# Two RMS norms of a decoder block: their sums over partitions taken by 32x32 block turns on VectorE instead of by products with ones

## The chip, the cores and the metric

The kernel runs on one core of a Trainium2 chip. The metric is the time of one execution in microseconds (us). The engines that matter here: PE (TensorE, matrix products; PEld is its loading of weights), DVE (VectorE), ACT (ScalarE), POOL (GpSimd) and SP (SyncE, which here only issues DMAs). All engines run on their own and in program order, and wait for each other by semaphores.

## What is computed

One decoder block over 256 tokens with a model width of 1024. Two of its steps are RMS norms over the width, one ahead of the attention part and one ahead of the gated feed-forward part (FFN). The reference, cut to that:

```python
def rms_norm(x, g):
    y = x * lax.rsqrt(jnp.mean(x * x, axis=-1, keepdims=True) + NORM_EPS)
    return y * g

h = rms_norm(x, attn_norm_g)
proj = jnp.einsum('bsd,de->bse', h, w_in)       # q, k, v of two attentions, forget, gates
...                                             # MoBA and FoX attention, gated merge
x = x + jnp.einsum('bsd,de->bse', merged, w_out)
h2 = rms_norm(x, ffn_norm_g)
up = jnp.einsum('bsd,df->bsf', h2, w_ffn_up)    # 1024 -> 2 x 2816
u, g = jnp.split(up, 2, axis=-1)
g = causal_depthwise_conv(g, ffn_conv_w, ffn_conv_b)
x = x + jnp.einsum('bsf,fd->bsd', jax.nn.silu(g) * u, w_ffn_down)
```

## The kernel before, in words

**Layout.** x lies transposed: the width on partitions (8 tiles of 128), the 256 tokens along the free axis. A norm therefore needs a sum over partitions. The gain g is multiplied into x early; the factor 1/sqrt(mean square) of a token is a scale of the result, so it is applied to what the products leave in PSUM. No product waits for it; what reads PSUM does.

**Three products for one.** Every large product is made in fp32r with both operands split into a high and a low part: hi*hi, lo*hi and hi*lo. ACT writes the high part of a weight (tile `whi`), DVE the low part (`wlo`); `load` records both for one "unit", which is half of a 1 MB weight chunk. SP fetches the chunks into `raw`, three buffers deep: a chunk's load is issued once DVE has made both low parts of the chunk three before it. PE uses the units in a fixed order; the splits run some five units ahead (six buffers each of `whi` and `wlo`).

**What sets the order.** PE's order is that of the code. For the other engines a scheduler sets it at build time from priorities (`soon`) and from extra orderings that `after` adds. A DMA that SP or POOL issues runs on the same 16 DMA engines.

**First norm.** ACT squares the tiles of x, POOL adds them up into `xss`, and `norm1_sums` splits the sum in two and multiplies it with a matrix of ones (two matmuls, L251), which leaves each token's sum on all partitions. `norm1` picks the diagonal (L257), works out the factor on 128x2 elements (`rsqrt_mean`, L228 to L232: DVE, ACT twice, DVE three times), turns it to rows (L262) and has POOL write those to DRAM and read them back spread over all partitions as `rsB` (L265, L266). The factor by token (`rs`) scales q, k and v; `rsB` scales the gates (L561).

**Second norm.** While the product with w_out ends (L680 to L682), DVE adds the residual (L685), ACT squares (L691), and POOL adds up `sqs` (L693 to L696). ACT and POOL split `sqs` (L700, L701). The function `norm2` stands inside `up(1)`, between matmuls: two products with ones (L714, L715) leave the sum of each token on all 128 partitions, and `rsqrt_mean` works out the factor `rs2` on 128x256 elements, already where it is used.

**FFN.** `up(f)` makes 48 matmuls of u and g of one 128-wide slice f into one of the eight PSUM banks. `finish_up(f)` reads it with `rs2` (L723), then convolution (ACT L727, DVE L728 and L729), SiLU (ACT L730), product with u (DVE L733) and the split for the next product (ACT L737, DVE L738) into `qT`, `kT` or `aT` by turns. `down(p)` multiplies slices 2p and 2p+1 with w_down. PE's order is up(0), up(1), up(2), up(3), down(0), up(4), up(5), down(1) and so on. `down` holds five banks from its first use to the end.

Of the kernel before, what the change touches and what calls it, by code (L numbers as in the profile page):

```python
# [8 lines left out]
F32 = mybir.dt.float32  # L9
# [3 lines left out]
ALU = mybir.AluOpType  # L13
# [31 lines left out]
def decoder_block(ctx, tc, a, out):  # L45
# [7 lines left out]
    def T(shape, tag, bufs=1, dt=F32):  # L53
        return sb.tile(shape, dt, tag=tag, bufs=bufs, name=tag)
# [4 lines left out]
    def bank():  # L59
        return ps.tile([P, 512], F32, tag="bank", bufs=8, name="bank")  # L60
# [33 lines left out]
    split = {}  # L94
    loads = {}
    rs_done = []
    first_lo = []
    state = {"next": 0, "raw": None, "lag": 0, "hi": None, "lo": None}

    def after(i, j):  # L100
# [2 lines left out]
    def load(upto):  # L103
        while state["next"] <= min(upto, len(units) - 1):
            c, h = units[state["next"]]
            if c[0] == "head":
                k = c[1]
                if k < 2:
                    raw = gates[:, 4 * k:4 * k + 4].rearrange("p a b t -> p (a b t)")
                    for s0, s1 in ((0, HX + W4), (HX + W4, HEADW)):  # L110
                        loads[c] = nc.sync.dma_start(raw[:, s0:s1], a["head"][k][:, s0:s1])
                    x, g, raw = raw[:, 0:S], raw[:, S:S + 1], raw[:, HX:HEADW]
                    nc.gpsimd.tensor_copy(xT[:, k], x)
                else:
                    if k % 2 == 0:
                        state["raw"] = T([P, 2048], "raw", RB)
                    raw = state["raw"][:, k % 2 * 1024:(k % 2 + 1) * 1024]
                    x, g = xT[:, k], g1[:, k:k + 1]
                    nc.sync.dma_start(x, a["head"][k][:, 0:S])
                    loads[c] = nc.sync.dma_start(raw, a["head"][k][:, HX:HEADW])  # L120
                xlo = split_x(k, x, g)
                at, n = 44, 2 if k < 2 else 1
            else:
                at, n = 44 if c[0] == "qkv" else 0, 1
                if h == 0:
                    src = a[c[0]]
                    for j in c[1:]:
                        src = src[j]
                    state["raw"] = T([P, 2048], "raw", RB)
                    loads[c] = nc.sync.dma_start(state["raw"], src)  # L130
                raw = state["raw"][:, h * 1024:(h + 1) * 1024]
            hi = T([P, 1088], "whi", HB, F32R)[:, at:at + 1024]
            lo = T([P, 1088], "wlo", HB, F32R)[:, at:at + 1024]
            w = 1024 // n
            for j in range(n):
                s = slice(j * w, (j + 1) * w)
                i = nc.scalar.activation(hi[:, s], raw[:, s], AF.Copy)  # L137
                d = nc.vector.tensor_tensor(lo[:, s], raw[:, s], hi[:, s].bitcast(F32), op=ALU.subtract)  # L138
                if (c, h) == (("qkv", 1, 1), 0):
                    after(i, rs_done[0])  # L140
                    after(d, rs_done[1])
                if (c, h) == (("qkv", 1, 0), 0):
                    first_lo.append(d)
                if c[0] == "head" and j == 0:
                    after(d, xlo)
                for this, last in ((i, state["hi"]), (d, state["lo"])):
                    if last is not None:
                        after(this, last)
            if c[0] == "head":
                square_x(k, x, i)  # L150
            split[c, h] = (hi, lo)
            state["last"] = i, d
            state["next"] += 1
# [49 lines left out]
    load(5)  # L203
    cst = T([P, 840], "cst")
    ident = cst[:, 0:128]
    ones = cst[:, 256:384]
    mask3 = cst[:, 384:768]
    cos2 = cst[:, 768:832].rearrange("p (t c) -> p t c", t=NT)
    sel = cst[:, 832:840]
    wfr = T([P, KT, NH], "wfr")  # L210
    wfg = T([P, KT, 32], "wfg")
    nc.gpsimd.memset(wfg, 0.0)
    gq = T([P, 2], "gq")

    casts = []

    def tables():
        for t, n in ((sm, "smalls"), (cst, "consts"), (wfr, "wf")):
            after(nc.sync.dma_start(t, a[n]), loads["head", KT - 1])
        nc.gpsimd.memset(first_ones.bitcast(F32), 1.0)  # L220
        nc.vector.tensor_scalar_mul(gq, sm[:, C_QG:C_QG + 4:2], -HD ** -0.5)
        nc.vector.tensor_tensor(wfg[:, :, 0:NH], wfr, g1[:, :, None].to_broadcast([P, KT, NH]), op=ALU.mult)

    def rsqrt_mean(dst, ss, n, shape, tag, bufs=2):

        w = T([P, 3] + shape, tag, bufs)
        v, y, t = w[:, 0], w[:, 1], w[:, 2]
        nc.vector.tensor_scalar(v, ss, 1.0 / n, EPS, op0=ALU.mult, op1=ALU.add)  # L228
        i = nc.scalar.activation(t, v, AF.Ln), nc.scalar.activation(y, t, AF.Exp, scale=-0.5)
        nc.vector.scalar_tensor_tensor(t, v, -0.5, y, op0=ALU.mult, op1=ALU.mult)  # L230
        nc.vector.tensor_tensor(t, t, y, op=ALU.mult)
        d = nc.vector.scalar_tensor_tensor(dst, t, 1.5, y, op0=ALU.add, op1=ALU.mult)  # L232
        return i + (d,)

    rsw = T([P, 32], "rsw")
    nc.gpsimd.memset(rsw, 0.0)
    rs = rsw[:, 0:NT]
    rsB = T([P, S], "rsB")
    rope = []
    flat = T16(4, "aT")  # L240

    first_ones = flat[:, 3, P:2 * P]

    def norm1_sums():
        nc.scalar.activation(flat[:, 0], xss[:, 1], AF.Copy)
        low = nc.gpsimd.tensor_tensor(flat[:, 1], xss[:, 1], flat[:, 0].bitcast(F32), op=ALU.subtract)
        for i in casts:
            after(i, low)
        ssp = wp[:, 0:S]
        for i in range(2):  # L250
            nc.tensor.matmul(ssp, first_ones, flat[:, i], start=(i == 0), stop=(i == 1))  # L251
        return ssp

    def norm1(ssp):
        ss1 = T([P, NT], "ss1")
        for t in range(NT):
            i = nc.vector.tensor_tensor_reduce(T([P, 512], "sq", 2)[:, 0:P], ssp[:, t * P:(t + 1) * P], ident, scale=1.0, scalar=0.0,  # L257
                                               op0=ALU.mult, op1=ALU.add, accum_out=ss1[:, t:t + 1])
            after(i, first_lo[0])
        rs_done.extend(rsqrt_mean(rs, ss1, D, [NT], "rsv")[1:])  # L260
        rsT = T([P, 32], "rsT")
        nc.vector.transpose(rsT, rsw)  # L262
        rd = dr.tile([NT, P], F32, name="rd")
        for t in range(NT):
            nc.gpsimd.dma_start(rd[t].rearrange("(i p) -> i p", p=32), rsT[t:P:32])  # L265
        nc.gpsimd.dma_start(rsB, bass.AP(tensor=rd.tensor, offset=rd.offset, ap=[[0, P], [1, S]]))  # L266

        for i in range(2):
            gr = sm[:, C_GR + 16 * i:C_GR + 16 * (i + 1)][:, None, :].to_broadcast([P, NT, 16])
            rc = T([P, NT, 16], f"rc{i}")  # L270
            rsn = T([P, NT, 16], f"rsn{i}")
            nc.vector.tensor_tensor(rc, cos2[:, :, 0:16], gr, op=ALU.mult)
            nc.vector.tensor_tensor(rsn, cos2[:, :, 16:32], gr, op=ALU.mult)
            rope.append((rc, rsn))
# [304 lines left out]
    for k in range(KT):  # L579
        if k == KT - 1:  # L580
            with soon():
                ssp = norm1_sums()
                norm1(ssp)
        project_qk(k, (pq, pk))
        if k == 2:
            tables()
# [84 lines left out]
    for c in range(4):  # L671
        for h in range(2):
# [10 lines left out]
            if c >= 2:  # L683
# [8 lines left out]
                if j == 0:  # L692
                    nc.gpsimd.tensor_tensor(sqs, sq[:, 0], sq[:, 1], op=ALU.add)  # L693
                else:
                    nc.gpsimd.tensor_tensor(sqs, sqs, sq[:, 0], op=ALU.add)
                    nc.gpsimd.tensor_tensor(sqs, sqs, sq[:, 1], op=ALU.add)  # L696
    sqr = T([P, NH, 384], "bias", 1, F32R)
    sqh, sql, ones_r = sqr[:, 0, 0:S], sqr[:, 1, 0:S], sqr[:, 2, 0:P]
    nc.gpsimd.tensor_copy(ones_r, ones)
    nc.scalar.activation(sqh, sqs, AF.Copy)  # L700
    nc.gpsimd.tensor_tensor(sql, sqs, sqh.bitcast(F32), op=ALU.subtract)  # L701
    sp = bank()
    rs2 = T([P, S], "rs2")


    acts = {}

    def up(f):
        up_ = bank()
        twin("wu", f, up_, hh, hl, f == 0, norm2 if f == 1 else None)  # L710
        return up_

    def norm2():
        nc.tensor.matmul(sp[:, 0:S], ones_r, sqh, start=True, stop=False)  # L714
        nc.tensor.matmul(sp[:, 0:S], ones_r, sql, start=False, stop=True)  # L715
        i = rsqrt_mean(rs2, sp[:, 0:S], D, [S], "s", 4)
        after(i[0], tables[0])
        tables.append(nc.scalar.preload_act_table_set("silu_and_others"))
        after(tables[1], i[1])

    def finish_up(f, up_):
        ev = T([P, 2, S], "sq", 2)
# [121 lines left out]
```

## Time and profile before

| | before |
|---|---|
| time, median of 3 runs | 360.86 us (360.52 to 361.11) |
| the profiled execution | 361.65 us, of which the span from first to last instruction is 359.9 us |
| mean granted TensorE clock | 0.997 |
| DVE, ACT, POOL busy | 75%, 62%, 11% of the span |
| HBM read | 66.75 MB, 188 GB/s over the span |

In a group's row stand line, engine, operation, tiles written<-read, shape, count, and after the bar the busy time and the mean of one in ns. In a timeline's row stand the start and the length in us, then engine, line and operation; behind it in brackets the engine's idle time before it and what ended that. A PE row's length includes the pipeline's depth; the distance of two starts is what a matmul takes of PE.

### The profile page before, as it was taken

To read this page: it belongs to the slowest core of one execution; us is meant where nothing else is said; L and a number is where in the kernel's file an instruction comes from. 1 tells how busy PE (TensorE), PEld (TensorE's weight loads), DVE (VectorE), ACT (ScalarE), POOL (GpSimd) and SP (SyncE) were. 2 spreads that over 40 slices of the span, in tenths; PEclk is the share of its full clock that TensorE was granted. 3 is DMA by queue.
4 is the path that set the end of the run, shared out by engine and by line. 5 is a ranking of instruction groups with operands and counts; after the bars stand their busy time and mean duration, and the time that the engine had idled before them with its cause. 6 is when DMAs were issued, how large, how long until landed. Compare 5 with 4: busy or idle time off the path is not lost.

```text
span 359.9 us, 7545 instructions
## 1 busy us (share of the span) xinstructions
PE 354.6 (99%) x3117; PEld 337.9 (94%) x3117; DVE 271.0 (75%) x463; ACT 221.5 (62%) x376; POOL 39.9 (11%) x54
## 2 busy tenths in 40 slices
PE   9999999999999999999999999999999999999995
PEld 5888899888899999999999999999999999999995
DVE  5899669798995558875969776868676776768643
ACT  5859656799894995545877654555464555555420
POOL 2442051430410000000530000000000000000000
PEclk9999999999999999999999999999999999999998
DMA  8986634557348335565464564564564564563003
GB/s 270 403 323 236 207 158 176 178 219 250 117 136 335 118 118 177 181 229 201 152 228 168 192 235 164 188 233 153 201 232 157 198 229 138 217 211 143 0 2 117
DMA packets 12130, 68.28 MB, mean 190 GB/s; under 512 B 1688, under 2 KB 2848, under 8 KB 4672
## 3 DMA queue, kind: packets, MB, share of 16 engines
q1 hardware_dynamic: 11664, 66.62, 51.4%
q0 software_dynamic: 288, 1.19, 0.8%
q8 instruction: 24, 0.39, 0.4%
q14 instruction: 10, 0.08, 0.1%
q10 hardware_dynamic: 144, 0.00, 0.0%
HBM read 66.75 MB, written 1.06 MB: 188 GB/s over the span
## 4 chain that ended last, share of the span: by engine, by line
PE 99%; issue 0%; DVE 0%
PE bank L551 15%; PE bank L552 15%; PE bank L553 15%; PE bank L299 12%; PE bank L285 6%; PE bank L757 6%; PE bank L758 6%; PE bank L756 6%; PE bank L682 2%; PE bank L656 2%; PE bank L681 2%; PE bank L680 2%; PE bank L655 2%; PE bank L654 2%; PE bank L520 1%; PE bank L445 1%
## 5 line engine op out<-in xcount | busy, mean ns | idle before, releaser
L138 DVE TENSOR_TENSOR wlo<-raw,whi 128x1024 fp32r<-128x1024 f32 x120 | 147.1, 1232 | 46.1 <-ACT whi L137 46.0
L137 ACT ACTIVATE whi<-raw 128x1024 fp32r<-128x1024 f32 x120 | 125.5, 1058 | 67.5 <-PE bank L552 39.5
L553 PE MATMUL bank<-oh,wlo 128*128 128x256 f32 x352 | 96.8, 275 | 0.0
L551 PE MATMUL bank<-oh,whi 128*128 128x256 f32 x352 | 96.8, 275 | 0.0
L552 PE MATMUL bank<-ol,whi 128*128 128x256 f32 x352 | 96.8, 275 | 0.0
L551 PEld LDWEIGHTS bank<-oh,whi 128*128 128x128 f32 x352 | 66.1, 188 | 0.0
L552 PEld LDWEIGHTS bank<-ol,whi 128*128 128x128 f32 x352 | 66.1, 188 | 0.0
L553 PEld LDWEIGHTS bank<-oh,wlo 128*128 128x128 f32 x352 | 66.1, 188 | 0.0
L552 PE MATMUL bank<-xl,whi 128*128 128x256 f32 x128 | 35.4, 276 | 0.4 <-issue 0.4
L551 PE MATMUL bank<-xh,whi 128*128 128x256 f32 x128 | 35.6, 278 | 0.0
L553 PE MATMUL bank<-xh,wlo 128*128 128x256 f32 x128 | 35.3, 276 | 0.0
L552 PEld LDWEIGHTS bank<-xl,whi 128*128 128x128 f32 x128 | 24.0, 188 | 0.8 <-issue 0.6
L551 PEld LDWEIGHTS bank<-xh,whi 128*128 128x128 f32 x128 | 24.0, 188 | 0.3
L553 PEld LDWEIGHTS bank<-xh,wlo 128*128 128x128 f32 x128 | 24.0, 188 | 0.0
L299 PE MATMUL bank<-whi,xh 128*128 128x512 f32 x64 | 21.2, 391 | 0.0
L299 PE MATMUL bank<-wlo,xh 128*128 128x512 f32 x64 | 21.0, 388 | 0.0
L299 PE MATMUL bank<-whi,xl 128*128 128x512 f32 x64 | 20.9, 388 | 0.0
L723 DVE TENSOR_TENSOR sq<-bank,rs 128x512 f32<-128x512 f32 x22 | 15.1, 691 | 6.6 <-PE bank L553 6.5
L654 PE MATMUL bank<-oh,whi 128*128 128x256 f32 x64 | 17.6, 275 | 0.0
L655 PE MATMUL bank<-ol,whi 128*128 128x256 f32 x64 | 17.6, 275 | 0.0
L656 PE MATMUL bank<-oh,wlo 128*128 128x256 f32 x64 | 17.6, 275 | 0.0
L680 PE MATMUL bank<-xh,whi 128*128 128x256 f32 x64 | 17.6, 275 | 0.0
(197 smaller groups left out, 754.6 us busy)
## 6 DMA issues: line engine op xcount, KB each, us to landing
raw<-in_wu SPq DMA_DIRECT2D x22, 1024.0 KB, 4.8
raw<-in_wd SPq DMA_DIRECT2D x11, 1024.0 KB, 4.8
raw<-in_qkv SPq DMA_DIRECT2D x8, 1024.0 KB, 5.1
raw<-in_wg SPq DMA_DIRECT2D x8, 1024.0 KB, 5.0
raw<-in_wb SPq DMA_DIRECT2D x4, 1024.0 KB, 4.9
raw<-in_wo SPq DMA_DIRECT2D x4, 1024.0 KB, 4.8
raw<-in_head SPq DMA_DIRECT2D x6, 512.0 KB, 6.6
gates<-cd POOLq DMA_DIRECT2D x1, 1024.0 KB, 6.9
```

Source lines behind the costliest of these rows:

```text
L137: i = nc.scalar.activation(hi[:, s], raw[:, s], AF.Copy)
L138: d = nc.vector.tensor_tensor(lo[:, s], raw[:, s], hi[:, s].bitcast(F32), op=ALU.subtract)
L285: nc.tensor.matmul(pt[t], lhs[:, k, t * P:(t + 1) * P], rhs, start=(k == 0 and i == 0), stop=(k == KT - 1 and i == 2))
L299: nc.tensor.matmul(pt[t], lhs[:, k, t * P:(t + 1) * P], rhs[:, c], start=(k == 0 and i == 0), stop=(k == KT - 1 and i == 2))
L551: nc.tensor.matmul(o, wh[:, w], mh[:, k], start=(k == 0 and i == 0), stop=False)
L552: nc.tensor.matmul(o, wh[:, w], ml[:, k], start=False, stop=False)
L553: nc.tensor.matmul(o, wl[:, w], mh[:, k], start=False, stop=(k == KT - 1 and i == 1))
L654: nc.tensor.matmul(o, wh[:, w], oh[:, 4 * br + k], start=(k == 0), stop=False)
L655: nc.tensor.matmul(o, wh[:, w], ol[:, 4 * br + k], start=False, stop=False)
L656: nc.tensor.matmul(o, wl[:, w], oh[:, 4 * br + k], start=False, stop=(k == 3))
L680: nc.tensor.matmul(o, wh[:, w], mh[:, k], start=(k == 0 and i == 0), stop=False)
L756: nc.tensor.matmul(o, wh[:, w], ah, start=(p == 0 and h == 0 and c == 0), stop=False)
```

## The change

Both norms get a new function `token_norm`. It turns the 128x256 sum in blocks of 32x32 on DVE (`turned`), so that tokens lie on partitions within each block; reduces over 32 (`part`, 128x8); copies the four groups of 32 partitions side by side (`four`, four copies of 32x8); reduces over the four (`total`, 32x8); works out the factor on 32x8; turns it to rows (`rows`); and has POOL write them to DRAM and read them back over all partitions. The matmuls with ones and the splits ahead of them go. In the first norm four more copies bring the factor into `rs`. In the second the last two additions into `sqs` move from POOL to DVE, the row `rs2` comes by way of DRAM, and the code stands ahead of `up(0)` instead of inside `up(1)`.

```diff
-    def norm1_sums():
-        nc.scalar.activation(flat[:, 0], xss[:, 1], AF.Copy)
-        low = nc.gpsimd.tensor_tensor(flat[:, 1], xss[:, 1], flat[:, 0].bitcast(F32), op=ALU.subtract)
-        ssp = wp[:, 0:S]
-        for i in range(2):
-            nc.tensor.matmul(ssp, first_ones, flat[:, i], start=(i == 0), stop=(i == 1))
-        return ssp
...
+    def token_norm(xx, row):
+        turned = T([P, S], "turned")
+        nc.vector.transpose(turned, xx)
+        part = T([P, NH], "part")
+        nc.vector.tensor_reduce(part, turned.rearrange("p (b t) -> p b t", t=32), axis=AX.X, op=ALU.add)
+        four = T([32, NH, 4], "four")
+        for q in range(4):
+            nc.vector.tensor_copy(four[:, :, q], part[32 * q:32 * (q + 1)])
+        total = T([32, NH], "total")
+        nc.vector.tensor_reduce(total, four, axis=AX.X, op=ALU.add)
+        i = rsqrt_mean(rst[:, 0:NH], total, D, [NH], "rsv", rows=32)
+        rows = T([32, 32], "rows")
+        nc.vector.transpose(rows, rst)
+        rd = dr.tile([NH, 32], F32, name="rd")
+        nc.gpsimd.dma_start(rd, rows[0:NH])
+        nc.gpsimd.dma_start(row, bass.AP(tensor=rd.tensor, offset=rd.offset, ap=[[0, P], [1, S]]))
+        return i
...
+    def norm1():
+        i = token_norm(xss[:, 1], rsB)
+        for q in range(4):
+            d = nc.vector.tensor_copy(rs[32 * q:32 * (q + 1)], rst[:, q:NH:4])
+        rs_done.extend((i[1], d))
...
-                    nc.gpsimd.tensor_tensor(sqs, sqs, sq[:, 0], op=ALU.add)
-                    nc.gpsimd.tensor_tensor(sqs, sqs, sq[:, 1], op=ALU.add)
-    sqr = T([P, NH, 384], "bias", 1, F32R)
-    sqh, sql, ones_r = sqr[:, 0, 0:S], sqr[:, 1, 0:S], sqr[:, 2, 0:P]
-    nc.gpsimd.tensor_copy(ones_r, ones)
-    nc.scalar.activation(sqh, sqs, AF.Copy)
-    nc.gpsimd.tensor_tensor(sql, sqs, sqh.bitcast(F32), op=ALU.subtract)
-    sp = bank()
+                    for b in range(2):
+                        (nc.vector if j == 3 else nc.gpsimd).tensor_tensor(sqs, sqs, sq[:, b], op=ALU.add)
     rs2 = T([P, S], "rs2")
+    i = token_norm(sqs, rs2)
+    after(i[0], tables[0])
+    tables.append(nc.scalar.preload_act_table_set("silu_and_others"))
+    after(tables[1], i[1])
...
-    def norm2():
-        nc.tensor.matmul(sp[:, 0:S], ones_r, sqh, start=True, stop=False)
-        nc.tensor.matmul(sp[:, 0:S], ones_r, sql, start=False, stop=True)
-        i = rsqrt_mean(rs2, sp[:, 0:S], D, [S], "s", 4)
```

Line numbers in the program after are lower by 1 to 22 for the same code. On DVE at the first norm the rows before are these; the two low parts (`wlo`) belong to the two units that PE takes up first after the head chunks:

```order
L138 TENSOR_TENSOR wlo<-raw,whi 128x1024
L257 ISA sq,ss_320<-bank,cst 128x128
L257 ISA ss_320 128x1
L257 ISA sq,ss_320<-bank,cst 128x128
L257 ISA ss_320 128x1
L138 TENSOR_TENSOR wlo<-raw,whi 128x1024
L228 TENSOR_SCALAR rsv<-ss_320 128x2
L230 SCALAR_TENSOR_TENSOR rsv<-rsv 128x2
L231 TENSOR_TENSOR rsv<-rsv 128x2
L232 SCALAR_TENSOR_TENSOR rsw<-rsv 128x2
L262 STREAM_TRANSPOSE rsT<-rsw 128x32
```

In the program after, both stand behind the whole norm, and two small products for the rotation (`rc`, `rsn`) between its steps:

```order
L237 COPY four<-part 32x8 x4
L261 TENSOR_TENSOR rc_346<-cst,sm 128x32
L262 TENSOR_TENSOR rsn_347<-cst,sm 128x32
L239 TENSOR_REDUCE total<-four 32x8
L220 TENSOR_SCALAR rsv<-total 32x8
L222 SCALAR_TENSOR_TENSOR rsv<-rsv 32x8
L223 TENSOR_TENSOR rsv<-rsv 32x8
L224 SCALAR_TENSOR_TENSOR rst<-rsv 32x8
L242 STREAM_TRANSPOSE rows<-rst 32x32
L254 COPY rs<-rst 32x2 x4
L137 TENSOR_TENSOR wlo<-raw,whi 128x1024 x2
```

On DVE at the second norm, from the reduction of the turned blocks to the first reading of the FFN's banks (`sq<-bank,rs`), in the program after; `turned` and one low part stand just ahead of it:

```order
L234 TENSOR_REDUCE part<-turned 128x8
L237 COPY four<-part 32x8 x4
L239 TENSOR_REDUCE total<-four 32x8
L220 TENSOR_SCALAR rsv<-total 32x8
L137 TENSOR_TENSOR wlo<-raw,whi 128x1024
L222 SCALAR_TENSOR_TENSOR rsv<-rsv 32x8
L223 TENSOR_TENSOR rsv<-rsv 32x8
L224 SCALAR_TENSOR_TENSOR rst<-rsv 32x8
L242 STREAM_TRANSPOSE rows<-rst 32x32
L137 TENSOR_TENSOR wlo<-raw,whi 128x1024 x2
L701 TENSOR_TENSOR sq<-bank,rs_2354 128x512 x2
L137 TENSOR_TENSOR wlo<-raw,whi 128x1024
```

The reading of the banks stands two low parts behind the turned rows, and waits there for the DMA. On POOL, ahead of the end of its program (before):

```order
L693 TENSOR_TENSOR sqs<-sq 128x256
L695 TENSOR_TENSOR sqs<-sqs,sq 128x256
L696 TENSOR_TENSOR sqs<-sqs,sq 128x256
L695 TENSOR_TENSOR sqs<-sqs,sq 128x256
L696 TENSOR_TENSOR sqs<-sqs,sq 128x256
L695 TENSOR_TENSOR sqs<-sqs,sq 128x256
L696 TENSOR_TENSOR sqs<-sqs,sq 128x256
L701 TENSOR_TENSOR bias<-sqs,bias 128x256
```

The same place in the program after, with two scalings of attention probabilities (`ol`) ahead of it:

```order
L471 TENSOR_TENSOR ol<-ol,r 128x2x128
L471 TENSOR_TENSOR ol<-ol,r 128x2x256
L681 TENSOR_TENSOR sqs<-sq 128x256
L684 TENSOR_TENSOR sqs<-sqs,sq 128x256 x4
L244 DMA rd<-rows 8x32
L245 DMA rs_2354<-rd 128x256
```

Two additions and the split have gone from POOL, and a write and a read of DRAM have come. PE's order is the same but for the four matmuls that have gone.

More of the change, by code (lines that the diff above doesn't have):

```diff
@@ L96, in decoder_block @@
     rs_done = []
-    first_lo = []
     state = {"next": 0, "raw": None, "lag": 0, "hi": None, "lo": None}
@@ L141, in load @@
                     after(d, rs_done[1])
-                if (c, h) == (("qkv", 1, 0), 0):
-                    first_lo.append(d)
                 if c[0] == "head" and j == 0:
@@ L205, in decoder_block @@
     ident = cst[:, 0:128]
-    ones = cst[:, 256:384]
     mask3 = cst[:, 384:768]
     cos2 = cst[:, 768:832].rearrange("p (t c) -> p t c", t=NT)
-    sel = cst[:, 832:840]
     wfr = T([P, KT, NH], "wfr")
@@ L213, in decoder_block @@
     gq = T([P, 2], "gq")
-    casts = []
     def tables():
@@ L219, in tables, with rsqrt_mean @@
             after(nc.sync.dma_start(t, a[n]), loads["head", KT - 1])
-        nc.gpsimd.memset(first_ones.bitcast(F32), 1.0)
         nc.vector.tensor_scalar_mul(gq, sm[:, C_QG:C_QG + 4:2], -HD ** -0.5)
         nc.vector.tensor_tensor(wfg[:, :, 0:NH], wfr, g1[:, :, None].to_broadcast([P, KT, NH]), op=ALU.mult)
-    def rsqrt_mean(dst, ss, n, shape, tag, bufs=2):
-        w = T([P, 3] + shape, tag, bufs)
+    def rsqrt_mean(dst, ss, n, shape, tag, bufs=2, rows=P):
+        w = T([P, 3] + shape, tag, bufs)[:rows]
         v, y, t = w[:, 0], w[:, 1], w[:, 2]
@@ L233, in rsqrt_mean @@
         return i + (d,)
-    rsw = T([P, 32], "rsw")
-    nc.gpsimd.memset(rsw, 0.0)
-    rs = rsw[:, 0:NT]
+    rs = T([P, NT], "rs")
     rsB = T([P, S], "rsB")
     rope = []
-    flat = T16(4, "aT")
-    first_ones = flat[:, 3, P:2 * P]
-    def norm1_sums():
-        nc.scalar.activation(flat[:, 0], xss[:, 1], AF.Copy)
-        low = nc.gpsimd.tensor_tensor(flat[:, 1], xss[:, 1], flat[:, 0].bitcast(F32), op=ALU.subtract)
-        for i in casts:
-            after(i, low)
-        ssp = wp[:, 0:S]
-        for i in range(2):
-            nc.tensor.matmul(ssp, first_ones, flat[:, i], start=(i == 0), stop=(i == 1))
-        return ssp
@@ L254, in norm1 @@
[L254 to L266, printed above, removed]
+    def token_norm(xx, row):
[15 more added lines that the diff above has]
+        return i
@@ L268, in norm1 @@
+    rst = T([32, 32], "rst")
+    nc.gpsimd.memset(rst, 0.0)
+    def norm1():
[3 more added lines that the diff above has]
+        rs_done.extend((i[1], d))
         for i in range(2):
@@ L581, in decoder_block @@
             with soon():
-                ssp = norm1_sums()
-                norm1(ssp)
+                norm1()
         project_qk(k, (pq, pk))
@@ L709, in up @@
         up_ = bank()
-        twin("wu", f, up_, hh, hl, f == 0, norm2 if f == 1 else None)
+        twin("wu", f, up_, hh, hl, f == 0)
         return up_
-    def norm2():
-        nc.tensor.matmul(sp[:, 0:S], ones_r, sqh, start=True, stop=False)
-        nc.tensor.matmul(sp[:, 0:S], ones_r, sql, start=False, stop=True)
-        i = rsqrt_mean(rs2, sp[:, 0:S], D, [S], "s", 4)
-        after(i[0], tables[0])
-        tables.append(nc.scalar.preload_act_table_set("silu_and_others"))
-        after(tables[1], i[1])
     def finish_up(f, up_):
```

## The prediction

> **What bounds the kernel now.** I read the page's busy shares first, then the chain that ended last, then PE's own waits, and last the timeline around the two norms.
>
> ```profile
> PE 354.6 (99%) x3117; PEld 337.9 (94%) x3117; DVE 271.0 (75%) x463; ACT 221.5 (62%) x376; POOL 39.9 (11%) x54
> ...
> PE 99%; issue 0%; DVE 0%
> ```
>
> ```profile
> PE bank L552 <- issue: 0.4, 1, 0.4
> ```
>
> PE is busy for 99% of the span, the chain that ended last is PE for 99%, and the only pause after the start is 0.4 us. So two things change the time, one for one: matmuls taken from PE, and a pause put into it. Work on DVE, ACT or POOL costs nothing until PE waits for it.
>
> **What goes: four matmuls.**
>
> ```profile
> 24.56 0.40 PE L251 MATMUL bank<-aT 128*128 128x256 f32 x2
> 24.80 0.63 PE L285 MATMUL bank<-whi,xh 128*128 128x512 f32 x2
> ...
> 184.35 0.28 PE L714 MATMUL bank<-bias 128*128 128x256 f32 x1
> 184.47 0.28 PE L715 MATMUL bank<-bias 128*128 128x256 f32 x1
> 184.59 0.28 PE L551 MATMUL bank<-oh,whi 128*128 128x256 f32 x1
> ```
>
> From the pair's start to the next matmul it is 24.80 - 24.56 = 0.24 us, and 184.59 - 184.35 = 0.24 us at the second norm: together -0.48 us. The splits taken from ACT and POOL hide under PE already, so they bring nothing.
>
> **First norm: a longer chain on DVE ahead of a low part that PE needs.**
>
> ```profile
> 21.39 1.21 DVE L138 TENSOR_TENSOR wlo<-raw,whi 128x1024 fp32r<-128x1024 f32 x1
> ...
> 23.42 0.18 DVE L272 TENSOR_TENSOR rc<-cst,sm 128x32 f32<-128x32 f32 x1
> 23.52 0.18 DVE L273 TENSOR_TENSOR rsn<-cst,sm 128x32 f32<-128x32 f32 x1
> ...
> 27.62 0.16 DVE L232 SCALAR_TENSOR_TENSOR rsw<-rsv 128x2 f32<-128x2 f32 x1
> 27.82 0.21 DVE L262 STREAM_TRANSPOSE rsT<-rsw 128x32 f32<-128x32 f32 x1
> ...
> 55.58 0.68 DVE L561 TENSOR_TENSOR gates<-bank,rsB 128x512 f32<-128x512 f32 x1
> ...
> 72.44 0.43 DVE L407 STREAM_TRANSPOSE cU<-cW 32x256 f32<-32x256 f32 x1
> ```
>
> ```profile
> L316 DVE TENSOR_REDUCE ss<-sq 128x8 f32<-128x512 f32 x8 | 5.1, 681 | 4.1 <-ACT sq L315 4.1
> ```
>
> ```profile
> 26.76 0.44 ACT L229 ACTIVATE rsv<-rsv 128x2 f32<-128x2 f32 x2 [3.29 <-DVE rsv L228]
> ```
>
> ```profile
> 28.00 0.39 PE L299 MATMUL bank<-wlo,xh 128*128 128x512 f32 x1
> ```
>
> Small independent operations start 0.10 us apart (23.42, 23.52), dependent ones 0.20 (27.62, 27.82). A turn of 256 columns is the L407 row, 0.43. The reduction of 256 has no row; it lies between the small operation's 0.18 and the 0.68 for 512, and I take 0.40, a little over half of the latter. A copy between groups of partitions has none either; I bound it by 0.10 and 0.20 and take 0.10, since the four do not depend on each other. DVE is free at 22.5 (21.39 + 1.21, less the overlap). Then: turn 0.45, reduction 0.40, eight small operations 0.80 (four copies and four products of the tables), sum and mean 0.40, ACT's two 0.50, three dependent steps 0.60, turned rows 0.10, four copies 0.40: 3.65. The low part starts at 26.2 and ends at 27.4. PE wants it at 28.00 - 0.24 = 27.76. The margin is 0.36 us, so I cost this at nothing; it is gone if all eight copies cost 0.20 (then 0.8 later, a pause of 0.45 us). The row `rsB` makes the same trip through DRAM as before, one write instead of two, some 2 us earlier; its first reader starts at 55.58, so that is free. SP's next loads are released up to 2 us later, with splits five units ahead of PE; free as well.
>
> **Second norm: when the row arrives.** Before, the factor needs no DMA.
>
> ```profile
> 178.93 0.62 ACT L691 ACTIVATE sq<-xT 128x512 f32<-128x512 f32 x1
> ```
>
> ```profile
> 179.13 0.87 DVE L689 SCALAR_TENSOR_TENSOR ol<-xT,sm,oh 128x256 fp32r<-128x256 f32 x2
> ```
>
> ```profile
> L661 DVE TENSOR_TENSOR sq<-sq 128x256 f32<-128x256 f32 x8 | 3.2, 417 | 0.1
> ```
>
> ACT's squares are there at 179.6, DVE is done with `ol` at 180.0. From there: two additions 0.9 (417 ns each and the handover), turn 0.45, a low part 1.2, reduction 0.40, copies 0.40, sum and mean 0.40, a low part 1.2 (ACT's two lie under it), three dependent steps 0.60, turned rows 0.20: 5.75, less some 0.15 of overlaps, so 185.6.
>
> ```profile
> 28.33 1.33 POOL L265 DMA_DIRECT2D rd<-rsT  x2 [5.12 <-DVE rsT L262]
> 33.01 0.58 POOL L266 DMA_DIRECT2D rsB<-rd  x1 [3.35 <-DMA rd<-rsT]
> ```
>
> ```profile
> rsB<-rd POOLq DMA_DIRECT2D x1, 128.0 KB, 4.0
> ...
> rd<-rsT POOLq DMA_DIRECT2D x2, 0.5 KB, 3.7
> ...
> cd<-cW POOLq DMA_DIRECT2D x1, 8.0 KB, 1.7
> ```
>
> ```profile
> 26.67 0.33 SPq L130 DMA_DIRECT2D raw<-in_qkv  x1
> 31.76 3.87 SPq L130 DMA_DIRECT2D raw<-in_wg  x2
> ...
> 185.04 0.33 SPq L130 DMA_DIRECT2D raw<-in_wu  x1
> 190.29 0.33 SPq L130 DMA_DIRECT2D raw<-in_wd  x1
> ```
>
> ```profile
> raw<-in_wu SPq DMA_DIRECT2D x22, 1024.0 KB, 4.8
> ```
>
> POOL issues 0.3 us after the turned rows (28.33 against 27.82 + 0.21), so at 185.9. The same trip in the first norm: 4.68 us from the first write's issue to the read's (28.33 to 33.01), of which the second write is 0.67, then 4.0 to the read's landing: 4.0 + 4.0 = 8.0. Both halves there run into a 1 MB load issued 1.7 and 1.3 us ahead of them (26.67, 31.76) and land just after it: at 4.8 for such a load, 31.5 against 32.0 for the write (28.33 + 3.7), and 36.6 against 37.0 for the read. `cd`, with no load near, takes 1.7. The second norm has the same neighbours. The load of `wu` at 185.04 is released by a low part that ends at 184.85 in the new order, one us ahead of the write; that of `wd` by the second low part behind the turned rows, between 188 and 190.3, so ahead of the read at about 190.5. With that issue in the middle, at 189.1, the load lands at 193.9 and the row 0.4 later, a trip of 8.4. I take 8.2, between the two: the row is there at 194.1. The bounds are 4.4 (both halves as `cd`, and 1.0 between them as from 32.0 to 33.01) and 9.6 (the load of `wd` at 190.3).
>
> ```profile
> 187.84 1.29 DVE L723 TENSOR_TENSOR sq<-bank,rs 128x512 f32<-128x512 f32 x2
> ...
> 194.16 1.22 DVE L138 TENSOR_TENSOR wlo<-raw,whi 128x1024 fp32r<-128x1024 f32 x1
> 195.30 0.75 DVE L738 TENSOR_TENSOR qT<-s,qT 128x256 fp32r<-128x256 f32 x2
> ```
>
> ```profile
> 198.01 0.28 PE L757 MATMUL bank<-qT,whi 128*128 128x256 f32 x1
> ```
>
> Behind the row: from the first bank read (187.84) to the end of the first slice's low part (195.30 + 0.42) it is 7.88 now, with a weights' low part (194.16 to 195.30) in it that now stands behind; that leaves 6.75. So `qT` is ready at 200.85. PE's second matmul of down(0) wants it at 198.01 - 0.24 = 197.77. PE pauses 200.85 - 197.77 = 3.1 us. Up to there up(0) to up(3) cover the wait: four banks besides the product's with w_out, so none of them needs a bank freed. Behind the waiting L723 on DVE stand the low parts of the unit that PE takes up after down(0), 48 matmuls or over 5 us later, and on ACT the FFN's scaling and the high parts of the same units; none is late. The second slice is needed 24 matmuls of some 0.12 us, 2.8 us, after the first, and comes 1.6 after it (a low part and its own 0.4). Later slices have their old slack, so this happens once. Decision point: the row at 191.0, a trip of 5.1 us.
>
> **What the pause does to PE's clock.**
>
> ```profile
> 0.78 4.00 PE L201 MATMUL bank<-const-bfloat16-1.0 128*128 128x512 bf16 x9 [0.78 <-PEq L837]
> 4.73 1.19 PE L285 MATMUL bank<-whi,xh 128*128 128x512 f32 x2
> ...
> 355.55 0.28 PE L758 MATMUL bank<-kT,wlo 128*128 128x256 f32 x1
> ```
>
> ```profile
> 356.00:358.00 2.00, 0.00 (x0) 0.00 (x0) 0.28 (x1) 0.00 (x0) 0.00 (x0) 0.95 0.76 262
> 358.00:360.00 2.00, 0.00 (x0) 0.00 (x0) 0.00 (x0) 0.00 (x0) 0.00 (x0) 0.50 0.00 0
> ```
>
> The last matmul ends at 355.83; the granted clock is 0.95 over the next stretch and then 0.50, so it halved at about 357.8, after 2.0 us without matmuls. A pause of 3.1 us is longer. What recovery costs has a bound in the start: two matmuls still take 1.19 us at 4.73, 4 us after PE began; so at most some 5.6 us at half speed, 2.8 us lost, and at least nothing. I take the middle, 1.4.
>
> **Sum.** -0.48 + 3.1 + 1.4 = +4.0 us. The profiled execution took 361.65 us (span 359.9 and 1.75 around it) and would take 365.7; it is 0.8 above the median, so on the median: 360.86 + 4.0 = 364.9. A change within 0.2% (0.7 us) counts as none.
>
> **Rivals.**
>
> - The clock holds. For it: nothing in this trace shows a pause within the kernel, only the end. Against: the 2.0 us there. 360.86 - 0.48 + 3.1 = 363.5. In the Trainium skill, "TensorE: Matmul & The Clock Gate", Part 1, the clock returns to half after at least one idle window of about 3.4 us; by that rule this rival holds, and the trace's end speaks against it.
> - The row comes in time: not slower. Both DMAs would have to get past the 1 MB loads and take what `cd` took: trip 4.4, below 5.1, no pause, 360.4. Against: neither half did in the first norm. The Trainium skill, "DMA: Bandwidth & Descriptors", section "Anatomy of one DMA", fits a GpSimd DMA as 2.0 us plus bytes over 436 GB/s, by which the trip is an estimated 5.3 us with the 1.0 between, the pause 0.2 and the time 360.6; `cd`'s 1.7 is near it, `rsB`'s 4.0 is not.
> - One half is caught by a load, one not: trip 8.2 - 2.3 = 5.9, pause 0.8, too short for the clock: 361.2.
> - It is worse: a trip of 9.6 (pause 4.5), the first norm's 0.45 on top, or the clock's full 2.8: 366 to 368.
>
> **Chances.** Forecast 0.45, clock holds 0.27, one half caught 0.12, in time 0.08, worse 0.08. The range leaves out "in time", most of "one half", and the far end of "worse": 361.8 to 366.6. Faster by over 0.2% needs more than the matmuls: 0.02; the same 0.13 ("in time" and part of "one half"); slower 0.85.
>
> **What the new profile would show.** Right: one idle stretch of PE near 197.5 to 200.8, at the first matmuls of down(0), ended by `qT`; L701's wait on DVE ended by the DMA of the row, POOL's two DMAs landing about 4 us after issue; granted clock about 0.5 for a few us behind it; no wait on PE near 27.8. Wrong: a row there by 191, which takes pause and clock with it; a wait on `wlo` near 27.8; or PE held longer because a bank or a weights' part is late after all.

## The result

The changed kernel takes 365.38 us (median of 6 executions, 363.74 to 366.39) against 360.78 us for the kernel before on the same chip: a ratio of 1.0127, 95% interval 1.0103 to 1.0152. It is 4.6 us slower; 364.9 was forecast. The profiled execution took 366.20 us.

The page's busy shares, its row of the granted clock and the chain that ended last, then PE's waits in total (engine, tile, line, what it waited for: us in total, times, longest):

```profile
PE 355.9 (98%) x3113; PEld 338.2 (93%) x3113; DVE 275.6 (76%) x480; ACT 220.1 (60%) x374; POOL 38.2 (10%) x49
...
PEclk9999999999999999999999899999999999999998
...
PE 89%; DVE 4%; DMA 2%; issue 1%; SPq 1%; ACT 1%; POOL 0%; DVEq 0%
```

```profile
PE bank L734 <- ACT qT L715: 2.5, 1, 2.5
...
PE bank L288 <- DVE wlo L137: 0.5, 1, 0.5
PE bank L735 <- DVE qT L716: 0.4, 1, 0.4
```

Before, the chain was PE for 99% and no pause was longer than 0.4 us. Now there are two pauses, one at each norm, and one slice in the middle of the clock's row is an 8 (the last slice, behind PE's work, is another). PE's other waits are 0.8 us on its own sequencer, at the start, and one of 0.2 us.

The first norm, DVE's rows and then PE's (start, length, engine, line; in brackets the idle time before):

```profile
23.43 0.69 DVE L237 COPY four<-part 32x8 f32<-32x8 f32 x4
...
25.94 0.64 DVE L254 COPY rs<-rst 32x2 f32<-32x2 f32 x4
26.61 2.36 DVE L137 TENSOR_TENSOR wlo<-raw,whi 128x1024 fp32r<-128x1024 f32 x2
```

```profile
26.95 0.39 PE L288 MATMUL bank<-whi,xl 128*128 128x512 f32 x1
27.88 0.50 PE L288 MATMUL bank<-wlo,xh 128*128 128x512 f32 x1 [0.54 <-DVE wlo L137]
```

At 0.23 us a matmul (before: 27.77 to 28.00) the second of these would have started at 27.18. It started at 27.88: 0.70 us lost in this execution.

The second norm on DVE, POOL, SP and PE:

```profile
185.21 0.20 DVE L242 STREAM_TRANSPOSE rows<-rst 32x32 f32<-32x32 f32 x1
...
194.05 1.29 DVE L701 TENSOR_TENSOR sq<-bank,rs 128x512 f32<-128x512 f32 x2 [5.20 <-DMA rs<-rd]
...
200.38 0.42 DVE L716 TENSOR_TENSOR qT<-s,qT 128x256 fp32r<-128x256 f32 x1
```

```profile
185.71 0.58 POOL L244 DMA_DIRECT2D rd<-rows  x1 [7.89 <-DVE rows L242]
190.12 0.57 POOL L245 DMA_DIRECT2D rs<-rd  x1 [3.84 <-DMA rd<-rows]
```

```profile
184.76 0.33 SPq L129 DMA_DIRECT2D raw<-in_wu  x1
188.88 0.33 SPq L129 DMA_DIRECT2D raw<-in_wd  x1
```

```profile
197.21 0.28 PE L542 MATMUL bank<-oh,wlo 128*128 128x256 f32 x1
200.03 0.38 PE L734 MATMUL bank<-qT,whi 128*128 128x256 f32 x1 [2.54 <-ACT qT L715]
200.85 0.38 PE L735 MATMUL bank<-qT,whi 128*128 128x256 f32 x1 [0.44 <-DVE qT L716]
```

The row's trip takes from 185.71 to 194.05, 8.3 us, and DVE stands still for 5.20 of it. PE's last matmul of up(3) starts at 197.21; two steps of 0.113 us later, at 197.44, the second matmul of down(0) was due. It starts at 200.85: 3.4 us lost.

The stretches around it (stretch, length, busy time of PE, PEld, DVE, ACT and POOL with the number of instructions, then the granted clock, the DMA engines' busy share and their GB/s):

```profile
198.00:200.00 2.00, 0.00 (x0) 0.00 (x0) 2.00 (x5) 1.01 (x4) 0.00 (x0) 1.00 0.00 0
202.00:204.00 2.00, 2.00 (x12) 2.00 (x11) 2.00 (x6) 1.13 (x2) 0.00 (x0) 0.53 0.70 291
204.00:206.00 2.00, 2.00 (x13) 2.00 (x12) 1.97 (x4) 1.05 (x4) 0.00 (x0) 0.61 0.02 4
```

While PE stands still the clock is full; it falls when PE is already at work again. The clock's records put the half-speed stretch at 202.14 to 205.55, 3.41 us, in which half the work is lost, 1.7 us. For this execution that makes -0.48 + 0.70 + 3.4 + 1.7 = +5.3, on the median of before 366.1, and 366.20 was measured. (The execution of before that was profiled, 361.65, lies 0.9 above its median, so against it the difference is only 4.55.)

### The profile page after: what moved, and what is told of

The parts are those of the page before. It is cut to its first block, busy times and chain, and to the rows that moved or that the text cites. A ratio compares the mean times of both kernels' runs of the same rounds, so it can differ in the third digit from the quotient of the medians.

```text
span 364.4 us, 7544 instructions
## 1 busy us (share of the span) xinstructions
PE 355.9 (98%) x3113; PEld 338.2 (93%) x3113; DVE 275.6 (76%) x480; ACT 220.1 (60%) x374; POOL 38.2 (10%) x49
## 4 chain that ended last, share of the span: by engine, by line
PE 89%; DVE 4%; DMA 2%; issue 1%; SPq 1%; ACT 1%; POOL 0%; DVEq 0%
PE bank L540 15%; PE bank L541 15%; PE bank L542 15%; PE bank L288 12%; PE bank L735 6%; PE bank L736 6%; PE bank L734 6%; PE bank L668 2%; PE bank L642 2%; PE bank L670 2%; PE bank L669 2%; PE bank L644 2%; PE bank L643 2%; DMA raw<-in_head 2%; DVE wlo L137 1%
## 5 line engine op out<-in xcount | busy, mean ns | idle before, releaser
L541 PE MATMUL bank<-ol,whi 128*128 128x256 f32 x352 | 96.8, 275 | 0.0
L542 PE MATMUL bank<-oh,wlo 128*128 128x256 f32 x352 | 96.8, 275 | 0.0
L540 PE MATMUL bank<-xh,whi 128*128 128x256 f32 x128 | 35.7, 279 | 0.2 <-issue 0.2
L734 PE MATMUL bank<-qT,whi 128*128 128x256 f32 x64 | 18.5, 288 | 2.5 <-ACT qT L715 2.5
L735 PE MATMUL bank<-qT,whi 128*128 128x256 f32 x64 | 18.4, 288 | 0.4 <-DVE qT L716 0.4
L736 PE MATMUL bank<-qT,wlo 128*128 128x256 f32 x64 | 18.4, 288 | 0.0
```

What stands on the lines that cost most here:

```text
L540: nc.tensor.matmul(o, wh[:, w], mh[:, k], start=(k == 0 and i == 0), stop=False)
L541: nc.tensor.matmul(o, wh[:, w], ml[:, k], start=False, stop=False)
L542: nc.tensor.matmul(o, wl[:, w], mh[:, k], start=False, stop=(k == KT - 1 and i == 1))
L734: nc.tensor.matmul(o, wh[:, w], ah, start=(p == 0 and h == 0 and c == 0), stop=False)
L735: nc.tensor.matmul(o, wh[:, w], al, start=False, stop=False)
L736: nc.tensor.matmul(o, wl[:, w], ah, start=False, stop=(last and h == 1 and d == ds[-1]))
```

## The experiments

Where a pause at down(0) is given below, it is worked out as above: the last start of up(3) plus two steps of 0.113, against the second matmul of down(0).

### Each norm alone

`n1_only` has the first norm of after and the second of before; `n2_only` the other way round.

```diff
 n1_only, against after:
-    i = token_norm(sqs, rs2)
+    nc.scalar.activation(sqh, sqs, AF.Copy)
+    nc.gpsimd.tensor_tensor(sql, sqs, sqh.bitcast(F32), op=ALU.subtract)
...
+        nc.tensor.matmul(sp[:, 0:S], ones_r, sqh, start=True, stop=False)
+        nc.tensor.matmul(sp[:, 0:S], ones_r, sql, start=False, stop=True)
...
 n2_only, against before:
-        nc.tensor.matmul(sp[:, 0:S], ones_r, sqh, start=True, stop=False)
-        nc.tensor.matmul(sp[:, 0:S], ones_r, sql, start=False, stop=True)
...
+    i = token_norm(sqs, rs2)
```

> Only the first norm is changed; the second is as before (products with ones). Theory: the new first norm costs a little, because its small copies start 0.18 us apart and the first low part is late: -0.24 us for the pair of matmuls, +0.70 us for the pause that the trace after shows at 27.9 (start to start), together +0.5: about 361.3, with one wait of PE on a low part of about 0.5 us near 27.8 and a granted clock of 1.0. Rival: the whole first norm is hidden, as was predicted, and the pause there is an accident of that execution: 360.5.

> Only the second norm is changed; the first is as before. Theory: the loss sits here: -0.24 us for the pair of matmuls, +3.4 us for PE's pause at down(0), and +1.6 us for half clock behind it in the executions in which the clock falls: 364.0 to 365.6. Rival: the first norm's longer chain carries a good part of the loss (later loads and splits), then this gives under 363.

`n1_only`: 361.45 us (360.95 to 362.01) against 360.89, ratio 1.0019 (1.0009 to 1.0029). `n2_only`: 365.05 us (363.97 to 367.00) against the same, ratio 1.0130 (1.0103 to 1.0156). PE's rows in `n1_only`, then in `n2_only`:

```profile
27.29 0.39 PE L289 MATMUL bank<-whi,xl 128*128 128x512 f32 x1
28.20 0.50 PE L289 MATMUL bank<-wlo,xh 128*128 128x512 f32 x1 [0.52 <-DVE wlo L137]
```

```profile
196.05 0.28 PE L574 MATMUL bank<-oh,wlo 128*128 128x256 f32 x1
199.02 0.52 PE L767 MATMUL bank<-qT,whi 128*128 128x256 f32 x1 [2.70 <-ACT qT L748]
199.84 0.58 PE L768 MATMUL bank<-qT,whi 128*128 128x256 f32 x1 [0.30 <-DVE qT L749]
```

The first norm is not free: its pause of 0.68 us is there without the second one's change, and -0.24 + 0.68 = +0.44 stands against 0.56 measured. The second norm carries nearly all of the loss; its pause is 3.56 us here.

The first norm's pause is not in every execution. `wide` and `sp_row`, described further below, keep the first norm of after, and their profiles show no such pause. In `wide`, DVE's low parts and the matmul of PE that takes up the first of them:

```profile
26.60 2.36 DVE L139 TENSOR_TENSOR wlo<-raw,whi 128x1024 fp32r<-128x1024 f32 x2
```

```profile
27.93 0.45 PE L294 MATMUL bank<-wlo,xh 128*128 128x512 f32 x1
```

The low part starts as it does in after (26.60 against 26.61), but PE comes to it at 27.93, where in after it was due at 27.18. The clock's records have the first rise to the full clock at 6.70 in `wide`, 6.30 in `sp_row`, and between 4.17 (after) and 5.99 in the seven profiles with this first norm that do have the pause, of 0.59 to 0.70 us. So what the first norm costs depends on when PE gets there; that the clock's first rise decides this is argued from these nine profiles, and no run varied it.

### The loads beside the trip

`hold` keeps DVE's chain and the two DMAs, and holds back the two loads that ran beside them:

```diff
+        if j == 1:
+            for n, c in enumerate((("wu", 3), ("wd", 0))):
+                nc.gpsimd.tensor_tensor(touched[:, n:n + 1], raws[c][:, 0:1], rs2[:, 0:1], op=ALU.add)
         v = up(2 * j + 1)
```

> The program after, with the two weight loads next to the row's trip held back until the row is there: POOL reads one column of the buffers that they are to overwrite, and adds the row's to it. DVE's chain is the same. Theory (the row's two DMAs are slow because each stands behind a 1 MB load): the write lands about 1.7 us after its issue and the read about 2 us after its own, the row is there by 190.7, PE does not wait at down(0), the clock stays at 1.0: 361.0 to 361.3. Rival (a write and a read by way of DRAM cost some 4 us each, whatever runs beside them): the same pause of 3.4 us and 365.4.

361.53 us (360.91 to 361.94), ratio 1.0014 (1.0005 to 1.0023). POOL's rows, DVE's reading of the row, PE at down(0):

```profile
185.81 0.56 POOL L247 DMA_DIRECT2D rd<-rows  x1 [7.89 <-DVE rows L245]
187.68 0.58 POOL L248 DMA_DIRECT2D rs<-rd  x1 [1.31 <-DMA rd<-rows]
```

```profile
190.95 1.29 DVE L705 TENSOR_TENSOR sq<-bank,rs 128x512 f32<-128x512 f32 x2 [1.99 <-DMA rs<-rd]
```

```profile
197.32 0.28 PE L545 MATMUL bank<-oh,wlo 128*128 128x256 f32 x1
197.43 0.28 PE L738 MATMUL bank<-qT,whi 128*128 128x256 f32 x1
197.74 0.39 PE L739 MATMUL bank<-qT,whi 128*128 128x256 f32 x1
```

With no load beside it the write costs 1.9 us up to the read's issue in place of 4.4, the read 3.3 in place of 3.9, the trip 5.1 in place of 8.3. The pause shrinks to 0.2 us. So the loads make the loss, mostly by way of the write: the read was expected at 2 us and takes 3.3 even alone. The packet records of the two runs show how. In after, the write waits 3.1 us after its issue: its packets begin at 188.77, when the load's large packets, from 185.74 on, come to their end (189.28). The read's packets there run from 193.01 to 193.72, again when a load's end (193.21). In `hold` they start 1.35 us after the issue, but run for 1.6 us, 189.03 to 190.62.

The Trainium skill, "DMA: Bandwidth & Descriptors", section "Queues, rings and completion order", says that a DMA engine drains a whole packet, typically 9 to 17 descriptors, from one queue before it turns to the next. The trace of after agrees with it as far as it goes: the 1 MB load is 128 records of 8 KB, which is 8 for each of 16 engines, and POOL's packets came as those ended. The records don't name the engine of a packet.

### What the read costs by itself

`wide` is `hold` with a read of 128 different rows instead of the same row 128 times. What it reads are constants, so the second norm's factor is left out of the result.

```diff
-        nc.gpsimd.dma_start(rd, rows[0:NH])
-        nc.gpsimd.dma_start(row, bass.AP(tensor=rd.tensor, offset=rd.offset, ap=[[0, P], [1, S]]))
+        wrote = nc.gpsimd.dma_start(rd, rows[0:NH])
+        if row is rsB:
+            nc.gpsimd.dma_start(row, bass.AP(tensor=rd.tensor, offset=rd.offset, ap=[[0, P], [1, S]]))
+        else:
+            after(nc.gpsimd.dma_start(row, a["consts"][:, 0:S]), wrote)
```

> The program with the loads held back, but the second norm's read fetches 128 different rows of 1 KB from the constants in place of 128 times the same 1 KB, and goes out right behind the write (the row is not the norm's then, so the output is not the block's). Only the read's landing is asked for. Theory (the read's 3.3 us are long because all copies come from one place: its packets took 0.3 to 0.4 us each and 1.6 us in all): 2.4 us. Rival (3.3 us is what a read of 128 KB issued by POOL costs): 3.3 us.

```profile
185.85 0.58 POOL L251 DMA_DIRECT2D rs<-in_consts  x1
```

```profile
188.45 1.29 DVE L708 TENSOR_TENSOR sq<-bank,rs 128x512 f32<-128x512 f32 x2 [1.16 <-DMA rs<-in_consts]
```

2.6 us from issue to use, and the packets take 0.8 us instead of 1.6: 0.7 us less than in `hold`, nearer to the theory's 2.4 than to the rival's 3.3. (The program's time is 360.95 us, ratio 1.0004, 0.9994 to 1.0015.) That the copies of one row are the reason is not shown. The same 128 copies take 0.7 us in after (193.01 to 193.72), where they run among the load's last packets; they take 1.6 us in `hold` and `best2`, where no load runs beside them. `wide` also reads another tensor, which was not written just before. Which of these makes the 0.7 us stays open.

### The clock

`fill` and `fill29` put matmuls into PE's wait, 22 and 29 of them; `after_again` is the program after, unchanged:

```diff
+        if j == 1:
+            for _ in range(FILL):
+                nc.tensor.matmul(acc[0][:, 0:S], hh[:, 0, 0:P], hl[:, 0], start=True, stop=True)
         if j > 0:
             down(j - 1)
```

> The program after, with 22 matmuls of 128x256 that nobody reads put in front of down(0), into the bank that down(0) then starts afresh; at 0.113 us each they fill 2.5 us of PE's wait. Theory (the clock halves because PE stood still): about 0.9 us of pause is left, too short, the granted clock stays at 1.0 in every run, and the time is 363.8 with little spread. Rival (the half-speed stretch, which began 1.3 us after PE had gone on, has another cause): it stays, and the time is 365.4 as before.

> The program after with 29 matmuls that nobody reads ahead of down(0), at 0.113 us the whole pause of 3.3 us, so that PE hardly stands still. Theory: the pause's time is lost as before, the clock keeps at 1.0, and the time is that of the run with 22 such matmuls, 364.4, with little spread and some 0.9 below the program after. Rival (the clock's part is nothing): the same time as the program after beside it.

> The program after, once more, beside the next one. Theory: the pause is 3.3 to 3.4 us in every execution, and the half clock behind it takes none, one or two stretches of 3.41 us, 1.7 us each: a spread from 363.7 to 367, with the mean granted clock falling as the time rises, and a middle near 365.3.

`fill`: 364.46 us (364.32 to 364.97) against 360.89, ratio 1.0105 (1.0089 to 1.0121). `fill29`: 364.70 (364.18 to 364.88); the program after beside it (`after_again`) 364.91 (364.03 to 367.61), both against 360.30, ratios 1.0119 (1.0103 to 1.0135) and 1.0118 (1.0099 to 1.0136). `fill29` in one of the stretches of above:

```profile
202.00:204.00 2.00, 2.00 (x20) 2.00 (x19) 2.00 (x5) 1.13 (x3) 0.00 (x0) 1.00 0.47 197
```

Medians do not tell `fill29` from after. The single executions do, with each one's mean granted clock:

| program | clock 0.999 or 1.000 | 0.992 to 0.995 | 0.988 |
|---|---|---|---|
| after, both times (11) | 363.74, 364.03, 364.71, 364.91, 365.22 | 365.33, 365.43, 365.67, 366.20, 366.39 | 367.61 |
| `n2_only` (6) | 363.97 | 364.61, 364.86, 365.25 | 366.42, 367.00 |
| `fill` and `fill29` (8) | 364.18 to 364.97 | none | none |

Of 11 executions of after the clock held in five, mean 364.5 us, which is what the filled programs take (mean 364.6). In five it lost one stretch, mean 365.8. The one at 0.988 was profiled: half clock from 200.05 to 206.88, two stretches. With PE kept busy it did not fall in any of 8. So the pause does bring the half clock, but not each time. In `fill` I had forgotten the first norm's 0.70 in the expected 363.8; with it, and the pause of 3.32 that its trace has, the sum is 360.89 - 0.48 + 0.70 + 3.32 = 364.43 against a median of 364.46.

### The order of the work

Three programs move things without taking any away. `early` puts two low parts behind the turned rows, `lowfirst` the copies of the first norm behind the first low part, `best` does both. In the diff `d` and `low` are low parts, and `i2[3]` is the turn of the rows:

```diff
 early:
+                if (c, h) == (("wu", 3), 0):
+                    after(d, i2[3])
 lowfirst:
-            nc.vector.tensor_copy(four[:, :, q], part[32 * q:32 * (q + 1)])
+            d = nc.vector.tensor_copy(four[:, :, q], part[32 * q:32 * (q + 1)])
+            if low is not None:
+                after(d, low)
```

> The program after, with the two low parts of the weights that DVE makes inside the second norm's chain (units of up(3), which PE needs some 10 us later) put behind the turned rows. Theory: the rows come 2.3 us earlier, at 182.9; the write goes out at 183.2, before the load that the later of these low parts releases; whatever the read then meets, the row is there by 189.5, ahead of the 190.7 that PE needs, so the pause at down(0) and the half clock go, and only the first norm's pause is left: -0.48 + 0.70 = +0.2, about 361.1. Rival (the trip waits out loads wherever it is put): the row comes no earlier than 193, and the time stays above 364.

> The program after, with the first norm's copies put behind the low part that PE needs first. Theory: the pause of 0.70 us near 27.9 goes, and nothing else changes: 364.7, with the pause at down(0) as before. Rival: the factor of the first norm comes 2.4 us later, the scaling of q and k with it, and PE waits for that or for a bank: 365.4 or more.

> Both orders together: the first norm's first low part ahead of its copies, and the second norm's chain ahead of two low parts. Theory: both pauses are gone and what is left is the four matmuls, -0.48 us: 360.4, a little under before, PE with no wait above 0.3 us. Rival: a later place pays for one of the moves: 361 or more.

`early`: 362.33 us (361.64 to 362.81) against 360.72, ratio 1.0041 (1.0026 to 1.0055). `lowfirst`: 365.53 (364.63 to 367.29), 1.0137 (1.0112 to 1.0162). `best`: 361.98 (361.07 to 362.16), 1.0026 (1.0015 to 1.0036).

POOL, SP and DVE in `early`, then in `best`:

```profile
184.40 0.58 POOL L247 DMA_DIRECT2D rd<-rows  x1 [6.37 <-DVE rows L245]
187.43 0.57 POOL L248 DMA_DIRECT2D rs<-rd  x1 [2.45 <-DMA rd<-rows]
```

```profile
186.97 0.33 SPq L130 DMA_DIRECT2D raw<-in_wu  x1
```

```profile
192.06 1.29 DVE L705 TENSOR_TENSOR sq<-bank,rs 128x512 f32<-128x512 f32 x2 [3.98 <-DMA rs<-rd]
```

```profile
185.25 0.57 POOL L252 DMA_DIRECT2D rs<-rd  x1 [1.85 <-DMA rd<-rows]
```

```profile
185.39 0.33 SPq L131 DMA_DIRECT2D raw<-in_wu  x1
```

```profile
190.51 1.29 DVE L709 TENSOR_TENSOR sq<-bank,rs 128x512 f32<-128x512 f32 x2 [4.01 <-DMA rs<-rd]
```

Neither theory of `early` held. Its rows come only 1.3 us earlier than in after, since one of the two low parts had covered ACT's turn, for which DVE now waits 0.5 us; and the read, with a load issued 0.46 us ahead of it, takes 4.6 us. The pause is 1.2 us. In `best` the load is issued 0.14 us behind the read and the read still loses, 5.3 us, as POOL's packets start only 1.35 us after the issue even alone (`hold`). Its pause is 1.2 us again, so the expected 360.4 was missed.

`lowfirst` takes the first pause away: the matmul that waited starts on time, 0.23 us behind the one before. Its time does not show it, because the clock fell in all five of its executions (0.988 to 0.995), and its median is no lower than after's. With one stretch lost its four executions have a mean of 365.4 us, where after's five have 365.8; that is too little to decide it.

`sp_row` issues the second norm's two DMAs on SP ahead of the next load (`i2[3]` is the read here):

```diff
-        nc.gpsimd.dma_start(rd, rows[0:NH])
+        nc.sync.dma_start(rd, rows[0:NH])
...
+                    if c == ("wu", 5):
+                        after(loads[c], i2[3])
```

> The program after, with the second norm's two DMAs issued by SP instead of POOL, ahead of the next weight load on SP's queue; the loads behind them come some 4 us later. DVE's chain is the same. Theory (what costs is to stand behind a 1 MB load): write 1.9 us, read between the 2.5 of SP's stores and the 3.3 that POOL's read took with the loads held back: the row by 190.5, pause at most 0.2, 361.1 to 361.5. Rival (the trip itself is long, some 8 us): 365.4.

```profile
184.69 0.35 SPq L248 DMA_DIRECT2D rd<-rows  x1
186.00 0.35 SPq L249 DMA_DIRECT2D rs<-rd  x1
186.45 0.38 SPq L130 DMA_DIRECT2D raw<-in_wu  x1
```

```profile
190.87 1.29 DVE L706 TENSOR_TENSOR sq<-bank,rs 128x512 f32<-128x512 f32 x2 [2.76 <-DMA rs<-rd]
```

362.20 us (361.78 to 363.14), ratio 1.0046 (1.0028 to 1.0065). The write costs 1.3 us, less than on POOL. The read takes 4.9. Its 128 packets of 1 KB begin at 186.97; 104 of them start ahead of the load's first packet (188.52), the others among the load's, and the last ends at 190.56. So to be ahead of the load on the same queue does not keep it apart; what SP's read takes with no load near was not measured. The pause at down(0) is 0.97 us, so the expected 361.1 to 361.5 was missed.

### Both orders, and the loads held back

`best2` is `best` with the hold of `hold`.

> The two orders together as in the run before, and the two loads held back until the row is there. Theory: the read meets no load and takes 3.3 us, the write went out behind the last load's end and takes 1.9 to 2.4: the row is there some 1.5 us before PE needs it. Neither pause is left, only the four matmuls are saved: -0.48 us, 360.3 against 360.8, a ratio of 0.9987. Rival: something else than these pauses (a start that differs, later loads) keeps it at 361 or above.

360.25 us (359.59 to 360.96) against 360.84, ratio 0.9982 (0.9973 to 0.9992).

```profile
185.97 0.59 POOL L253 DMA_DIRECT2D rs<-rd  x1 [2.11 <-DMA rd<-rows]
```

```profile
189.17 1.29 DVE L711 TENSOR_TENSOR sq<-bank,rs 128x512 f32<-128x512 f32 x2 [2.20 <-DMA rs<-rd]
```

```profile
PE 99%; DVE 0%; issue 0%
```

PE has no wait left but the start's, and the change is worth what its matmuls were, 0.6 us by the medians where 0.48 was expected. It beats both kernels, by little. The programs side by side, with the time that the pauses give (without the clock) and the measured difference of medians, in us:

| program | first pause | pause at down(0) | sum with the matmuls | measured |
|---|---|---|---|---|
| `n1_only` | 0.68 | 0 | +0.44 | +0.56 |
| `hold` | 0.60 | 0.19 | +0.3 | +0.64 |
| `early` | 0.7 | 1.19 | +1.4 | +1.61 |
| `best` | 0 | 1.20 | +0.7 | +1.26 |
| `sp_row` | 0 | 0.97 | +0.5 | +1.48 |
| `fill` | 0.7 | 3.32 | +3.5 | +3.57 |
| `best2` | 0 | 0 | -0.48 | -0.59 |

The pauses are those of the profiled execution, the measured difference is that of the medians. For `best` and `sp_row` the sum is 0.5 and 1.0 us short. Their profiled executions are the fastest of each (361.07 and 361.78 us), so the others may have longer pauses; no trace shows those.

## Why the prediction was right, and where not

The time, 365.4 against 364.9, came out right, and for the main reason given: the row comes too late for down(0), and loads make it late. That the total is within 0.5 us is in part luck, since terms were off in opposite directions.

- **The four matmuls, -0.48.** Right: `best2`, which has only that left, is 0.6 us faster than before.
- **First norm, nothing.** Wrong, it costs 0.70 in the profiled execution, where a wait on `wlo` near 27.8 had been named as a sign of being wrong. Two things used up the margin of 0.36. One is the eight copies at 0.10 us each. They cost 0.69 and 0.64 for four, where 0.40 was put down, though they do not depend on each other; close to the upper bound of 0.20 that the text named. The low part starts at 26.61 instead of 26.2, and PE can use it at 27.88, 0.1 behind the 27.76 at which PE was to want it. The larger part, 0.58, is that PE wanted it at 27.18. The 27.76 came from one execution of before, in which the clock first rose at 6.24; in the profile of after it rose at 4.17. In `wide` and `sp_row`, with a late rise, there is no pause. `n1_only` has a median 0.56 above before, so the pause is not a rare one.
- **DVE's chain to the rows, 185.6.** Right: 185.41. POOL issues at 185.71 (185.9).
- **The trip, 8.2.** Right in sum, 8.3, and in the cause that was given for its length: freed of the loads it is 5.1, so they make 3.2 of it. The low bound of 4.4 was wrong. It gave the read `cd`'s 1.7 us, and the row's read takes 3.3 in `hold` with no load beside it. So the rival "in time" had no room: at its best the trip is as long as the 5.1 that decided.
- **Row at 191.0 as the decision point.** `hold` has it at 190.95, and its pause is 0.2.
- **6.75 us from the row to `qT`.** Right: 194.05 to 200.80. The pause is 3.4 instead of 3.1 because PE was 0.3 us earlier at down(0).
- **The clock, 1.4.** That the pause can halve the clock is right. That it does so because it is longer than 2.0 us is not: in five of 11 executions of after the clock held, and their times have the whole pause in them. The size is an average that no execution has: nothing in those five, 1.7 us for each lost stretch in the others. The bound of 5.6 us at half speed does not come out of the two rows it was read from (4.73 + 1.19 - 0.78 = 5.1), and `after_again` has 6.83. In the first six executions the median lies 0.9 above that of `fill`. The rival "clock holds" (363.5, or 364.2 with the first norm's 0.70) is what those five executions show.
- **After the pause**, a slack that returns: right. No PE wait above 0.2 us follows, and nothing behind the waiting bank read came late.

In short, +0.70 was missed at the first norm and +0.3 at the pause, and the clock took about 0.5 less than put down.

## What to carry to other kernels

A small DMA on a latency path can cost what a large load beside it costs: here a write of 1 KB took 1.9 us alone and 4.4 behind 1 MB. So look up which load is issued within the microseconds around it, and either hold that load back, if it has slack, or keep the value on the chip. Where PE is the bound, count what a new wait has as cover in its own stage, in matmuls ahead of the first one that needs it, and take a margin of some tenths of a us from more than one execution: PE came to the same matmul 0.75 us apart in two profiles with the same first norm. Work that is short in elements is not short in time: four copies of 32x8 cost DVE 0.69 us, more than half of a 128x1024 subtraction (1.2).

## What the runs showed of the hardware that was not expected

- The clock changes on a grid. In the trace after it rises at 4.17, falls at 202.14 and rises at 205.55; 202.14 - 4.17 is 58 times 3.413 us. It fell after windows of that grid in which PE was busy for 49% (after), 29% (`after_again`) and 21% (`n2_only`) of the time, and no window was wholly idle. In the profile of after PE had been at work again for 1.3 us when it fell. One window busy for 45%, at the end of `hold`, did not halve it, so a threshold can't be read from these runs. The Trainium skill, "TensorE: Matmul & The Clock Gate", Part 1, has the window of 3.4 us and that it runs freely, which agrees with the grid; that it takes an idle window does not agree with these.
- The half-speed stretch is one or two windows long. In `after_again` and `lowfirst` PE was busy for 88% of the first slow window and the clock stayed low for a second (6.83 us in all); in `n2_only` it was busy for 91% and the clock rose after one.
- With no load beside it, a read of the same 1 KB row into 128 partitions took 1.6 us in its packets (`hold`, `best2`), a read of 128 rows 0.8 (`wide`); but among the last packets of a load the same 128 copies took 0.7 (after). The cause is open.
- A load issued 0.14 us behind a small read of POOL still overtakes it: the read takes 5.3 us, and 3.3 with no load near. A load behind a read on the same SP queue mixes with the read's last packets: 4.9 us from the read's issue to its use.
